# Feature-on-partition products with one 512-wide moving operand for both halves of the activation, group by group

## The chip, the core and the metric

The kernel runs on one core of a Trainium2 chip. The metric is the device time of one execution in microseconds, taken as the median of several runs. The core has a matrix engine (TensorE, PE in the profile; its weight loads are listed apart as PEld), a vector engine (VectorE, DVE), a scalar engine (ScalarE, ACT), GpSimd (POOL), and SyncE (SP), which only issues transfers here. Each engine runs its own instructions in the order in which they were written, and waits on semaphores for the others. Products land in PSUM banks of 128 partitions x 512 floats; everything else lies in SBUF.

## What is computed

Three layers on one sequence of 256 rows and 1024 features, all in float32. The first two are mixer plus MLP, the third is a hybrid of attention and convolution:

```
# layers 1 and 2
x = x + rmsnorm(mixer(rmsnorm(x, g0)), g1)          # HGRN2 + retention; then mLSTM
x = x + rmsnorm(square(relu(rmsnorm(x, g2) @ w1)) @ w2, g3)   # w1: 1024 x 4096
# layer 3
h = rmsnorm(x, g) * (1 + scale) + shift             # shift, scale, gate from silu(c) @ w_ada
q, k, v, g_attn, cb, cc, cx, g_conv, m_attn, m_conv = split(h @ w_in)   # 10 x 1024 columns
y_attn = (attention(q, k, v) * silu(g_attn)) @ w_o_attn
y_conv = (cb * conv(cc * cx) * silu(g_conv)) @ w_o_conv
out = rmsnorm(x + gate * ((sigmoid(m_attn) * y_attn + sigmoid(m_conv) * y_conv) @ w_out), final_g)
```

## The kernel before

Every large product is made exact enough by halves: an operand a is kept as hi (rounded to the format that PE multiplies in one pass, fp32r) and lo = a - hi, and a product is hi x hi + hi x lo + lo x hi, three matmuls that add up in one PSUM bank. Weights come from memory as raw tiles of 128 x 1024 floats (512 KB, five buffers, tag `raw`). Each is split into a **unit** (`u`, hi and lo, eight buffers): ACT copies raw to hi, DVE subtracts hi from raw for lo (`emit_split`). Most units hold 256 rows of a weight matrix by 512 columns.

There are two kinds of product.

- **A** (`mmA`, `blockA`, `stagA`, `out_stag`, `w2_block`): the activation is the stationary operand (128 x 128), the weights move with 512 columns, and rows of the sequence land on the partitions.
- **B** (`mmB`, `blockB`): the weights are stationary (128 x 128), the activation moves with its 256 rows, and features land on the partitions. A B block makes 512 output features from four units; its two banks hold two groups of 128 features each. There are 38 such blocks: two in the first mixer, six in each MLP, two in the second mixer, 22 in the third layer.

`blockB` goes unit by unit: for each unit, its two contraction steps `a`, and in each step the four groups `c`; `mmB` issues three matmuls of 256 columns. When the last unit is done, `evac(ps)` gets both banks. In the MLPs the banks come from the ring `ax` (four), elsewhere from `mm` (four). In the MLPs a B block is followed by a `w2_block` of kind A. The activations lie in the class `Act`: one tile for all hi, one for all lo, as [T, k, 128] (`tk`) or [k, 256] (`kt`).

What stands where in the program is decided by a planner at build time (`Sched`). It keeps one clock for each engine from cost figures given with each operation (109.0 ns for a B matmul, 216.3 for an A matmul), and starts pieces of other work ("jobs", generators that yield) between matmuls when their inputs should be ready. `pump` emits loads and splits ahead of their use, as long as raw and unit buffers are free; each unit has a due time from the sum of the costs that stand with `U(...)`.

Users of B blocks that the change touches: `evac_b` (relu squared in the MLPs), `l3_q`, `l3_k` and `attn` (attention), `conv_half`, `gate_block`, and `wo_conv`, whose activation was two four-step halves joined by `Both`. The first mixer's first B block (`ev_f`) follows a `stagA` stage; around it DVE and ACT also do a small softmax (`vec_job`), and DVE multiplies by the gain vector `ghg`, which is loaded late. In attention a head is scores (PE), then bias, maximum, exponential, sum and scaling (DVE, ACT), then transposes (PE), a copy (ACT), and the product with v (PE), all as a job between the matmuls of B blocks.

Of the kernel before, what the change touches and what calls it, by code (L numbers as in the profile page):

```python
# [34 lines left out]
LAST = -1.0  # L35
# [158 lines left out]
class Both:  # L194
    def __init__(self, a, b):
        self.a = (a, b)

    def r(self, i, kt):
        return self.a[kt // 4].r(i, kt % 4)
# [3 lines left out]
def tile_model(ctx: ExitStack, tc: tile.TileContext, I: dict, out: bass.AP, stop=None):  # L203
# [294 lines left out]
    def blockB(w, c0, act, evac, alloc=None, nk=8):  # L498

        us = units1(w, c0, 0, nk)  # L500
        ps = []

        def fn(j):
            def g(u):
                if j == 0:
                    ps.extend([(alloc or mmb)(), (alloc or mmb)()])
# [29 lines left out]
    def new_act8():  # L536
        return Act(a8(F32R), a8(F32R), "tk", 8)

# [43 lines left out]
    class Stage:  # L582
# [6 lines left out]
        def get(self):  # L589
            if self.act is None:  # L590
                self.act = new_act8()
# [432 lines left out]
    def mlp(l, stage, nxt, gpost, gpre, shift=None, ada=None):  # L1024
# [26 lines left out]
        def evac_b(b):  # L1051
            def evac(ps):
                def job():
                    Z[b] = z_tile(b)
                    for i in range(2):
                        r, s_ = s2(), s2()
                        A(r, ps[i], AF.Relu)
                        tt(s_, r, r, ALU.mult)
                        hi, lo = (Z[b].p[k][:, 2 * i:2 * i + 2, :].rearrange("p k c -> p (k c)") for k in range(2))
                        A(hi, r, AF.Square)  # L1060
# [385 lines left out]

    def l3_g(b):
# [10 lines left out]
    def l3_q(b):  # L1458
        def evac(ps):
            E3["q", b] = s4()  # L1460
            for i in range(2):
                A(E3["q", b][:, i * 512:i * 512 + 512], ps[i], AF.Copy, scale=128.0 ** -0.5)
        return evac

    def l3_k(b):
        def evac(ps):
            if b == 0:
                E3["oT"] = Act(a8(F32R), a8(F32R), "kt", 8)
            prev = E3.get("att")
            E3["att"] = sc.start(attn(b, prev, ps))  # L1470
        return evac

    def attn(b, prev, ps):
        E3["k", b] = s4()
# [305 lines left out]
```

## Time and profile before

| what | us |
|---|---|
| median of 3 runs | 989.31 (987.98 to 989.83) |
| the profiled execution | 986.43 |
| its span, first to last instruction | 984.6 |
| PE busy in the span | 967.7 |
| DVE busy | 669.8 |
| ACT busy | 541.1 |

The profiled execution is one run; its rows add up to its span, and 1.8 us lie outside the span. Busy times of an engine are unions, so a matmul whose drain overlaps the next counts once there, while "mean ns of one" includes the overlap. The pace of a stream is therefore read from the starts of successive pieces, not from that mean.

### The profile page before, as it was taken

To read this page: it belongs to the slowest core of one execution; us is meant where nothing else is said; L and a number is where in the kernel's file an instruction comes from. 1 tells how busy PE (TensorE), PEld (TensorE's weight loads), DVE (VectorE), ACT (ScalarE), POOL (GpSimd) and SP (SyncE) were. 2 spreads that over 40 slices of the span, in tenths; PEclk is the share of its full clock that TensorE was granted. 3 is DMA by queue.
4 is the path that set the end of the run, shared out by engine and by line. 5 is a ranking of instruction groups with operands and counts; after the bars stand their busy time and mean duration, and the time that the engine had idled before them with its cause. 6 is when DMAs were issued, how large, how long until landed. Compare 5 with 4: busy or idle time off the path is not lost.

```text
span 984.6 us, 15496 instructions
## 1 busy us (share of the span) xinstructions
PE 967.7 (98%) x6168; PEld 874.6 (89%) x6168; DVE 669.8 (68%) x885; ACT 541.1 (55%) x772; POOL 4.1 (0%) x11
## 2 busy tenths in 40 slices
PE   8999999999999999998999999999999999999997
PEld 6998888789989987987799999988999999999995
DVE  6689776775555547787888878658545577546564
ACT  7663565764554446766656544646545446444533
POOL 1000000000000000000000000000000000000000
PEclk9999999999999999999999999999999999999999
DMA  8670447566766546546679987626874426865531
GB/s 310 219 243 22 150 150 271 159 202 201 233 183 195 172 120 203 166 139 213 206 252 338 332 286 260 182 90 219 235 231 129 136 80 203 267 188 178 189 111 43
DMA packets 84316, 189.71 MB, mean 193 GB/s; under 512 B 7184, under 2 KB 9616, under 8 KB 84244
## 3 DMA queue, kind: packets, MB, share of 16 engines
q1 hardware_dynamic: 83956, 188.21, 59.8%
q8 instruction: 48, 0.79, 0.3%
q10 hardware_dynamic: 288, 0.52, 0.1%
q14 instruction: 24, 0.20, 0.1%
HBM read 187.46 MB, written 1.25 MB: 192 GB/s over the span
## 4 chain that ended last, share of the span: by engine, by line
PE 86%; DVE 7%; ACT 3%; issue 2%; DMA 2%; SPq 0%; DVEq 0%; ACTq 0%
PE mm L291 66%; PE ax L291 19%; DVE u L264 3%; DVE s L275 2%; PE ax L295 2%; DMA x<-in_x_dram 1%; ACT junk L260 1%; DMA raw<-in_mlp_w_dram 1%; DVE s L264 1%; DVE x L264 1%; ACT u L260 0%; SPq L306 0%; ACT s L260 0%; ACT L260 0%; DVE a L264 0%
## 5 line engine op out<-in xcount | busy, mean ns | idle before, releaser
L264 DVE TENSOR_TENSOR u<-raw,u 128x1024 fp32r<-128x1024 f32 x316 | 380.4, 1222 | 195.4 <-ACT u L260 194.2
L291 PE MATMUL mm<-u,a 128*128 128x512 f32 x1968 | 469.3, 394 | 4.5 <-ACT a L260 2.0
L260 ACT ACTIVATE u<-raw 128x1024 fp32r<-128x1024 f32 x316 | 328.6, 1055 | 230.7 <-PE mm L291 128.7
L291 PEld LDWEIGHTS mm<-u,a 128*128 128x128 f32 x1968 | 364.7, 188 | 83.1 <-DVE a L264 3.5
L291 PE MATMUL mm<-a,u 128*128 128x256 f32 x2496 | 305.3, 284 | 0.0
L291 PEld LDWEIGHTS mm<-a,u 128*128 128x128 f32 x2496 | 301.5, 192 | 0.6
L291 PEld LDWEIGHTS ax<-a,u 128*128 128x128 f32 x1152 | 139.9, 192 | 0.9
L291 PE MATMUL ax<-a,u 128*128 128x256 f32 x1152 | 140.6, 283 | 0.0
L260 ACT ACTIVATE s<-mm 128x512 f32<-128x512 f32 x64 | 36.4, 592 | 25.9 <-PE mm L291 25.1
L260 ACT ACTIVATE s<-ax 128x512 f32<-128x512 f32 (+1 forms) x43 | 24.5, 570 | 44.3 <-PE ax L295 23.6
L279 DVE RECIPROCAL sm<-sm 128x1 f32<-128x1 f32 (+2 forms) x43 | 7.0, 164 | 57.0 <-ACT sm L260 48.2
L260 ACT ACTIVATE a<-s 128x512 fp32r<-128x512 f32 (+1 forms) x37 | 23.8, 644 | 22.9 <-DVE s L264 22.1
L260 ACT ACT_TABLE_LOAD x27 | 34.6, 1283 | 2.3 <-DVE lbv L264 0.9
L264 DVE TENSOR_TENSOR s<-mm,s 128x512 f32<-128x512 f32 (+1 forms) x46 | 27.8, 637 | 12.0 <-PE mm L291 7.7
L295 PE MATMUL ax<-ident,s 128*128 128x128 f32 (+1 forms) x196 | 29.8, 273 | 4.4 <-DVE s L264 3.2
L295 PEld LDWEIGHTS ax<-ident,s 128*128 128x128 f32 (+1 forms) x196 | 23.1, 140 | 11.1 <-issue 4.4
L260 ACT ACTIVATE a<-ax 128x512 fp32r<-128x512 f32 x38 | 22.2, 595 | 19.1 <-PE ax L295 18.7
L264 DVE TENSOR_TENSOR a<-s,a 128x512 fp32r<-128x512 f32 x36 | 24.9, 692 | 11.3 <-ACT a L260 8.8
L264 DVE TENSOR_TENSOR s<-s,s 128x512 f32<-128x512 f32 (+4 forms) x42 | 28.9, 691 | 2.8 <-ACT s L260 2.0
L264 DVE TENSOR_TENSOR a<-ax,a 128x512 fp32r<-128x512 f32 x38 | 25.6, 686 | 7.1 <-ACT a L260 7.1
L291 PE MATMUL ax<-s,s 128*128 128x256 f32 (+2 forms) x156 | 29.9, 331 | 0.0
L275 DVE SCALAR_TENSOR_TENSOR s<-raw,silc,s 128x1024 f32<-128x1024 f32 x21 | 26.9, 1279 | 0.0
(98 smaller groups left out, 353.2 us busy)
## 6 DMA issues: line engine op xcount, KB each, us to landing
raw<-in_mlp_w_dram SPq DMA_DIRECT2D x128, 512.0 KB
raw<-in_w_in_dram SPq DMA_DIRECT2D x80, 512.0 KB
raw<-in_ev_w_in_dram SPq DMA_DIRECT2D x40, 512.0 KB
raw<-in_od_w_in_dram SPq DMA_DIRECT2D x24, 512.0 KB
raw<-in_w_ada_dram SPq DMA_DIRECT2D x24, 512.0 KB
raw<-in_ev_w_out_dram SPq DMA_DIRECT2D x12, 512.0 KB
s<-in_norm_g_dram SPq DMA_DIRECT2D x8, 512.0 KB
raw<-in_od_w_out_dram SPq DMA_DIRECT2D x8, 512.0 KB
```

Source lines behind the costliest of these rows:

```text
L260: nc.scalar.activation(o, i, f, **kw)
L264: (nc.vector if e == "v" else nc.gpsimd).tensor_tensor(out=o, in0=a, in1=b, op=op)
L275: nc.vector.scalar_tensor_tensor(out=o, in0=a, scalar=s, in1=b, op0=op0, op1=op1, **kw)
L279: nc.vector.reciprocal(o, i)
L291: nc.tensor.matmul(o, l, r, start=start, stop=stop_)
L295: nc.tensor.transpose(o, i, idt)
```

## The change

`Act` stays for the last product and for intermediate activations of kind A; a new class `Pair` replaces it (and `Both`) where B blocks read. It stores hi and lo of the same contraction step side by side, in tiles of four steps each, so that `both(kt)` is one operand of 512 columns: hi of 256 rows, then lo of 256 rows. `mmB` issues one matmul of 512 columns (hi weights against both halves, which fills a whole bank: hi x hi in its first 256 columns, hi x lo in the others) and one of 256 (lo weights against hi, into the first 256). `blockB` runs group by group: each of the four column groups has a bank of its own and runs through all four units. When a group ends, `hi_lo_sum` copies the second half of its bank to SBUF (ACT) and adds the first half (DVE). The evacuations then read sums in SBUF; those that were plain copies (q, k, cc) are gone, and the gates are taken in place. The factor of q moved into the DVE step that adds the bias to the scores. `evac_b` squares on DVE in the first MLP and on ACT in the second.

```
 class Pair:
+    def __init__(self, lay, tiles):
+        ...
+        form = "p (t k i c) -> p t k i c" if lay == "tk" else "p (k i c) -> p k i c"
+        dims = dict(t=2, k=4, i=2) if lay == "tk" else dict(k=4, i=2)
...
+    def both(self, kt):
+        p, k = self.p[kt // 4], kt % 4
+        if self.lay == "tk":
+            return p[:, :, k, :, :].rearrange("p t i c -> p i t c")
+        return p[:, k, :, :].rearrange("p i c -> p (i c)")
...
     def mmB(ps, act, kt, u, off, start, stop_):
         wh, wl = u[:, 0, off:off + 128], u[:, 1, off:off + 128]
-        mm(ps, wh, act.r(0, kt), start, False, 109.0)
-        mm(ps, wh, act.r(1, kt), False, False, 109.0)
-        mm(ps, wl, act.r(0, kt), False, stop_, 109.0)
+        if stop_:
+            mm(ps[:, 0:256], wl, act.r(0, kt), False, False, 120.0)
+        o = ps.rearrange("p (i t c) -> p i t c", i=2, t=2) if act.lay == "tk" else ps
+        mm(o, wh, act.both(kt), start, stop_, 226.5)
+        if not stop_:
+            mm(ps[:, 0:256], wl, act.r(0, kt), False, False, 120.0)
...
-    def blockB(w, c0, act, evac, alloc=None, nk=8):
+    def blockB(w, c0, act, evac, alloc=None, into=None):
...
+                if j == 0:
+                    ps[c] = (alloc or mmb)()
                 for a in range(2):
-                    for c in range(4):
-                        mmB(ps[c // 2][:, (c % 2) * 256:(c % 2) * 256 + 256], act(), 2 * j + a, u,
-                            a * 512 + c * 128, j == 0 and a == 0 and c % 2 == 0, j == nk // 2 - 1 and a == 1 and c % 2 == 1)
+                    mmB(ps[c], act(), 2 * j + a, u, a * 512 + c * 128, j == 0 and a == 0, j == 3 and a == 1)
             return g
-        for j in range(nk // 2):
-            U(us[j], fn(j), 2620.0)
-        F(lambda: evac(ps))
+        def add(c):
+            def f():
+                if c == 0 and into is not None:
+                    t = into()
+                    vs.extend([t[:, 0:512], t[:, 512:1024]])
+                elif c % 2 == 0 and into is None:
+                    vs.append(s2())
+                o = (c % 2) * 256
+                jobs.append(sc.start(hi_lo_sum(vs[c // 2][:, o:o + 256], ps[c], c == 3)))
+                if c == 3:
+                    for j in jobs:
+                        sc.finish(j)
+                    evac(vs)
+            return f
+
+        for c in range(4):
+            for j in range(4):
+                U(us[j], fn(c, j), 693.0)
+            F(add(c))
+
+    def hi_lo_sum(o, ps, now):
+        if not now:
+            yield
+        A(o, ps[:, 256:512])
+        if not now:
+            yield
+        tt(o, ps[:, 0:256], o, ALU.add)
+        yield LAST
...
-                        r, s_ = s2(), s2()
-                        A(r, ps[i], AF.Relu)
-                        tt(s_, r, r, ALU.mult)
+                        s_ = s2()
+                        if ada is None:
+                            stt(s_, ps[i], 0.0, ps[i], ALU.max, ALU.mult)
+                        else:
+                            A(s_, ps[i], AF.Relu)
+                            A(s_, s_, AF.Square)
...
-            tt(L[:, 0:128], sp[:, 0:128], bt[:, h, 128:256], ALU.add)
-            tt(L[:, 128:384], sp[:, 128:384], bt[:, h, :], ALU.add)
+            stt(L[:, 0:128], sp[:, 0:128], 128.0 ** -0.5, bt[:, h, 128:256], ALU.mult, ALU.add)
+            stt(L[:, 128:384], sp[:, 128:384], 128.0 ** -0.5, bt[:, h, :], ALU.mult, ALU.add)
...
-        blockB(w_in, 512 * b, y_in.get, l3_q(b))
-        blockB(w_in, 1024 + 512 * b, y_in.get, l3_k(b))
+        blockB(w_in, 512 * b, y_in.get, lambda ps: None, into=keep(("q", b)))
+        blockB(w_in, 1024 + 512 * b, y_in.get, l3_k(b), into=keep(("k", b)))
```

The instructions move as follows. On PE, at the start of the first mixer's first B block, before (`mm` banks, `u` units, `a` activation tiles; the numbers tell buffers apart):

```order
L291 MATMUL mm_368<-a_13_123,u_302 128x256 [waits Activation_49]
L291 MATMUL mm_368<-a_14_124,u_302 128x256
L291 MATMUL mm_368<-a_13_123,u_302 128x256 [waits DVE_49]
...
L291 MATMUL mm_369<-a_13_123,u_302 128x256 x2
L291 MATMUL mm_369<-a_14_124,u_302 128x256
...
L291 MATMUL mm_368<-a_13_123,u_337 128x256 [waits Activation_49]
L291 MATMUL mm_368<-a_14_124,u_337 128x256
L291 MATMUL mm_368<-a_13_123,u_337 128x256 [waits DVE_49]
```

and in the changed kernel:

```order
L319 MATMUL mm_373<-a_13_123,u_302 128x512 [waits Activation_49]
L319 MATMUL mm_373<-a_13_123,u_302 128x256 [waits DVE_49]
...
L319 MATMUL mm_373<-a_13_123,u_313 128x512 [waits Activation_49]
L319 MATMUL mm_373<-a_13_123,u_313 128x256 [waits DVE_49]
...
L319 MATMUL mm_373<-a_14_124,u_318 128x512 [waits Activation_49]
L319 MATMUL mm_373<-a_14_124,u_318 128x256 [waits DVE_49]
...
L319 MATMUL mm_373<-a_14_124,u_347 128x512 [waits Activation_49]
L319 MATMUL mm_373<-a_14_124,u_347 128x256 [waits DVE_49]
...
L319 MATMUL mm_391<-a_13_123,u_302 128x512
```

The second unit (u_337 before, u_313 now) is first read after 24 matmuls before and after four now, and the block's first bank reads all four units before its second bank begins.

On DVE around the small softmax of `vec_job` (`sm`, `vec`, `lbv`, `silc`), just ahead of that block, before:

```order
L264 TENSOR_TENSOR s_48_269<-s_48_269,ghg 128x512 [waits DMAHW0_49,DVE_49]
L264 TENSOR_TENSOR u_302<-raw_172,u_302 128x1024 [waits DMAHW5_49,Activation_49]
L264 TENSOR_TENSOR sm_318<-vec 128x4 [waits Activation_49]
...
L270 TENSOR_SCALAR lbv<-lbv 128x4 [waits DVE_49]
L264 TENSOR_TENSOR silc<-vec,sm_317 128x8 [waits Activation_49]
L264 TENSOR_TENSOR u_337<-raw_182,u_337 128x1024 [waits DMAHW6_49,PE_49,Activation_49]
L264 TENSOR_TENSOR u_354<-raw_205,u_354 128x1024 [waits DMAHW7_49,PE_49,Activation_49]
```

and in the changed kernel:

```order
L292 TENSOR_TENSOR s_48_269<-s_48_269,ghg 128x512 [waits DMAHW0_49,DVE_49]
L292 TENSOR_TENSOR u_302<-raw_172,u_302 128x1024 [waits DMAHW5_49,Activation_49]
L292 TENSOR_TENSOR u_313<-raw_182,u_313 128x1024 [waits DMAHW6_49,Activation_49]
L292 TENSOR_TENSOR u_318<-raw_205,u_318 128x1024 [waits DMAHW7_49,Activation_49]
L292 TENSOR_TENSOR sm_328<-vec 128x4 [waits Activation_49]
...
L292 TENSOR_TENSOR silc<-vec,sm_327 128x8 [waits Activation_49]
L292 TENSOR_TENSOR u_347<-raw_215,u_347 128x1024 [waits PE_49,Activation_49]
```

Two more splits stand ahead of the softmax now, and the block's fourth unit is the first behind it. ACT has its part in the same order: the hi copy of that unit comes after the second table load of the softmax.

On DVE in the third layer, around the first head of the second half of the heads (`s` from `ax`: scores plus bias), before:

```order
L264 TENSOR_TENSOR u_7211<-raw_6977,u_7211 128x1024
L264 TENSOR_TENSOR s_1079_7235<-ax_7232,a_987_6391 128x128
L264 TENSOR_TENSOR s_1079_7235<-ax_7232,a_987_6391 128x256
L287 TENSOR_REDUCE sm_7236<-s_1079_7235 128x1 x2
L270 TENSOR_SCALAR sm_7236<-sm_7236 128x2
```

and in the changed kernel:

```order
L292 TENSOR_TENSOR s_1115_6604<-mm_6587,s_1115_6604 128x256
L292 TENSOR_TENSOR u_6646<-raw_6506,u_6646 128x1024
L292 TENSOR_TENSOR u_6657<-raw_6515,u_6657 128x1024
L303 SCALAR_TENSOR_TENSOR s_1131_6678<-ax_6675,a_1025_6000 128x128
L303 SCALAR_TENSOR_TENSOR s_1131_6678<-ax_6675,a_1025_6000 128x256
L315 TENSOR_REDUCE sm_6679<-s_1131_6678 128x1 x2
L298 TENSOR_SCALAR sm_6679<-sm_6679 128x2
```

The sum of a group's two halves (the 128x256 row that reads `mm_6587`) and two splits stand ahead of the head's chain, where one split stood. Between this head's scores and its transposes PE has 18 matmuls of its B blocks in the changed kernel (nine of 512 and nine of 256), and 34 of 256 before.

## Rows read from the trace of the kernel before

**Rows 1.** The page: span, and busy time of each engine.
```profile
span 984.6 us, 15496 instructions
...
PE 967.7 (98%) x6168; PEld 874.6 (89%) x6168; DVE 669.8 (68%) x885; ACT 541.1 (55%) x772; POOL 4.1 (0%) x11
```
**Rows 2.** The page: the chain that ended last, shares by engine.
```profile
PE 86%; DVE 7%; ACT 3%; issue 2%; DMA 2%; SPq 0%; DVEq 0%; ACTq 0%
```
**Rows 3.** The chain from 223 to 258: start us, us, what (first MLP).
```profile
223.79 10.91 PE mm L291 x48
234.70 11.51 PE ax L291 x96
246.21 10.91 PE mm L291 x48
```
**Rows 4.** Costliest groups: xcount, busy us, mean ns of one, idle before.
```profile
L291 PE MATMUL mm<-a,u 128*128 128x256 f32 x2496 | 305.3, 284 | 0.0
...
L291 PE MATMUL ax<-a,u 128*128 128x256 f32 x1152 | 140.6, 283 | 0.0
```
**Rows 5.** Busy time of each engine in one B block, then clock, DMA share, GB/s.
```profile
234.55:246.05 11.50, 11.50 (x97) 11.50 (x96) 4.90 (x4) 4.23 (x4) 0.00 (x0) 1.00 0.71 213
```
**Rows 6.** The chain from 394 to 398: gate products, 36 weight columns, 256 moving.
```profile
394.53 2.77 PE ax L291 x24
```
**Rows 7.** PE busy in 20 us of tk blocks, and of kt blocks.
```profile
812.00:832.00 20.00, 20.00 (x169) 1.00 0.62 189
...
934.00:954.00 20.00, 20.00 (x169) 1.00 0.47 157
```
**Rows 8.** Timeline from 27 to 40, around the first B block's start.
```profile
28.96 0.69 DVE L264 TENSOR_TENSOR s<-s,ghg 128x512 f32<-128x512 f32 x1 [4.13 <-DMA ghg<-in_ev_hg_norm_g_dram]
...
29.57 1.22 DVE L264 TENSOR_TENSOR u<-raw,u 128x1024 fp32r<-128x1024 f32 x1
...
33.80 1.99 ACT L260 ACTIVATE u<-raw 128x1024 fp32r<-128x1024 f32 x2
...
34.36 5.92 PE L291 MATMUL mm<-a,u 128*128 128x256 f32 x48
34.87 2.36 DVE L264 TENSOR_TENSOR u<-raw,u 128x1024 fp32r<-128x1024 f32 x2 [0.78 <-ACT u L260]
```
**Rows 9.** Timeline from 504 to 507: the second MLP's first B block.
```profile
504.17 2.35 DVE L264 TENSOR_TENSOR u<-raw,u 128x1024 fp32r<-128x1024 f32 x2
...
505.36 1.83 PE L291 MATMUL ax<-a,u 128*128 128x256 f32 x14
```
**Rows 10.** Costliest groups, two rows; then engines' busy time from 700 to 800.
```profile
L264 DVE TENSOR_TENSOR s<-mm,s 128x512 f32<-128x512 f32 x38 | 25.1, 685 | 12.0 <-PE mm L291 7.7 <-ACT s L260 4.3
...
L260 ACT ACTIVATE junk<-ax 128x256 f32<-128x256 f32 x12 | 4.6, 385 | 5.8 <-PE ax L291 5.7
...
700.00:800.00 100.00, 100.00 (x819) 99.31 (x819) 55.44 (x98) 49.99 (x84) 0.00 (x0) 1.00 0.57 162
```
**Rows 11.** Timeline from 745 to 756: one head of attention.
```profile
746.96 0.49 ACT L260 ACTIVATE s<-ax 128x384 f32<-128x384 f32 x1 [2.76 <-PE ax L295]
...
749.20 4.77 PE L291 MATMUL mm<-a,u 128*128 128x256 f32 x37
749.59 0.62 DVE L264 TENSOR_TENSOR s<-ax,a 128x128 f32<-128x128 f32 x2
...
752.19 0.55 DVE L270 TENSOR_SCALAR s<-s,sm 128x128 f32<-128x128 f32 x2
```
**Rows 12.** Timeline from 451 to 462: PE's longest idle inside the program.
```profile
457.70 1.17 PE L295 MATMUL ax<-ident,s 128*128 128x128 f32 x8 [2.87 <-DVE s L264]
```
**Rows 13.** Timeline from 955 to 962: the last stage's start.
```profile
955.82 6.54 PE L291 MATMUL mm<-u,a 128*128 128x512 f32 x28
...
960.74 0.69 DVE L264 TENSOR_TENSOR a<-s,a 128x512 fp32r<-128x512 f32 x1 [0.70 <-ACT a L260]
```
**Rows 14.** Busy times in a stretch of the second MLP; the last two: DMA share, GB/s.
```profile
528.53:539.74 11.21, 11.21 (x96) 11.21 (x95) 9.18 (x8) 6.04 (x7) 0.00 (x0) 1.00 0.98 362
```

More of the change, by code (lines that the diff above doesn't have):

```diff
@@ L537, in new_act8, with new_pair8 @@
         return Act(a8(F32R), a8(F32R), "tk", 8)
+    def new_pair8(lay="tk"):
+        return Pair(lay, [a8(F32R), a8(F32R)])
     def to_act(src, act, T, k0, n):
@@ L590, in get @@
             if self.act is None:
-                self.act = new_act8()
+                self.act = new_pair8()
             return self.act
@@ L1445, in silu_fm, with keep, f @@
             tt(dst[:, c], ps[i], dst[:, c], ALU.mult)
+    def keep(key):
+        def f():
+            E3[key] = s4()
+            return E3[key]
+        return f
     def l3_g(b):
@@ L1456, in tile_model @@
         blockB(w_in, 3072 + 512 * b, y_in.get, l3_g(b))
[L1458 to L1463, printed above, removed]
     def l3_k(b):
@@ L1467, in evac, with attn @@
             if b == 0:
-                E3["oT"] = Act(a8(F32R), a8(F32R), "kt", 8)
+                E3["oT"] = new_pair8("kt")
             prev = E3.get("att")
-            E3["att"] = sc.start(attn(b, prev, ps))
+            E3["att"] = sc.start(attn(b, prev))
         return evac
-    def attn(b, prev, ps):
-        E3["k", b] = s4()
-        for i in range(2):
-            A(E3["k", b][:, i * 512:i * 512 + 512], ps[i])
+    def attn(b, prev):
         yield
@@ L1515, in attn @@
                 tt(ob, po, E3["g", b][:, (hh - 1) * 256:(hh + 1) * 256], ALU.mult)
-                hi, lo = (E3["oT"].p[i][:, h - 1:h + 1, :].rearrange("p k c -> p (k c)") for i in range(2))
+                hi, lo = (E3["oT"].f(i, h - 1, 2) for i in range(2))
+                ob = ob.rearrange("p (k c) -> p k c", k=2)
                 A(hi, ob)
@@ L1529, in cc @@
         def cc(ps):
-            K["u"] = s4()
-            for i in range(2):
-                A(K["u"][:, i * 512:i * 512 + 512], ps[i])
+            K["u"] = E3["u", b]
         def cx(ps):
@@ L1570, in job @@
                     k0 = 2 * i
-                    hi, lo = (act.p[n][:, k0:k0 + 2, :].rearrange("p k c -> p (k c)") for n in range(2))
-                    A(hi, g[:, c])
-                    tt(lo, g[:, c], hi.bitcast(F32), ALU.subtract)
+                    hi, lo = (act.f(n, k0, 2) for n in range(2))
+                    g3 = g[:, c].rearrange("p (k c) -> p k c", k=2)
+                    A(hi, g3)
+                    tt(lo, g3, hi.bitcast(F32), ALU.subtract)
                 yield LAST
@@ L1577, in conv_half @@
         for o, f in ((5120, cc), (6144, cx), (4096, cb), (7168, cg)):
-            blockB(w_in, o + 512 * b, y_in.get, f)
+            blockB(w_in, o + 512 * b, y_in.get, f, into=keep(("u", b)) if f is cc else None)
     def gate_block(key, o):
@@ L1582, in evac @@
             def evac(ps):
-                E3[key, b] = s4()
                 for i in range(2):
-                    A(E3[key, b][:, i * 512:i * 512 + 512], ps[i], AF.Sigmoid)
+                    A(ps[i], ps[i], AF.Sigmoid)
             return evac
         for b in range(2):
-            blockB(w_in, o + 512 * b, y_in.get, mk(b))
+            blockB(w_in, o + 512 * b, y_in.get, mk(b), into=keep((key, b)))
     def wo_attn(b):
```

35 lines of the change are left out of this document (23 added, 12 removed).

## The prediction

> **What bounds the kernel now.** I read the page's busy shares first: TensorE (PE) is busy 967.7 us of a span of 984.6 us, the vector engine (DVE) 68% and the scalar engine (ACT) 55% [rows 1]. The chain that ended last says the same: 86% of it is PE [rows 2]. So the time is PE's stream, and an edit pays if it shortens that stream or opens no new hole in it. PE's 16.9 us of idle lie mostly at the start and the end; between them one stall of 2.87 us in the second layer's mixer stands out, and comes up below.
>
> Next I took the chain over one piece of the MLP, where two kinds of stage alternate, so that the start of a piece to the start of the next is the pure pace. Activation-stationary products of 512 columns: 48 from 223.79 to 234.70, 10.91 us, 227.3 ns each. Feature-on-partition products (the kind the change touches, "B" below) of 256 columns: 96 from 234.70 to 246.21, 11.51 us, 119.9 ns each [rows 3]. The granted clock is 2.4 GHz there (1.00 of full speed), so 512 columns are 213.3 ns and 256 are 106.7: the pair of weight load and matmul costs 14.0 and 13.2 ns beyond its columns. There are 2496 + 1152 = 3648 such 256-column matmuls [rows 4], which is 38 B blocks of 96, or 1216 groups of three (one contraction step of one output bank).
>
> **The change part by part.** *The matmuls.* A group was hi x hi, hi x lo, lo x hi, three times 256 columns. It becomes one matmul of 512 (hi weights against both halves) and one of 256: the same 768 columns, one pair less. By the pure paces 3 x 119.9 = 359.7 ns becomes 227.3 + 119.9 = 347.2, so 12.5 ns a group and 1216 x 12.5 = 15.2 us in all. No row shows the two widths alternating, so both ends need a bound. Upper gain: if the weight load were wholly hidden behind the wide matmul, only columns remain, 768 / 2.4 = 320 ns, 39.7 ns a group, 48 us. Weight loads are busy 11.50 of 11.50 us in a B block [rows 5], which leaves that possible; but the stream of 24 gate products with only 36 weight columns still takes 2.77 us, 115.4 ns each, 8.7 beyond its columns [rows 6], so a shorter load takes away a third of the excess, not all. If both matmuls of a group paid only those 8.7 ns, a group would be 337.4 and the gain 22.3 ns, 27 us: there I put the upper end. Lower end: nothing saved, or a loss, if the wide moving operand is read more slowly than a plain one; in the stage layout it is four separate runs of 128 now, two before. Blocks with runs of 128 and blocks with one run of 256 keep the same pace, 169 matmuls touched in 20 us each [rows 7], so I expect no price. I take 12.5 because the pure 512 stream already has its load hidden behind a long matmul and still shows 14.0.
>
> Against that stands a rule: the Trainium skill, TensorE: Matmul & The Clock Gate, section "Back-to-back issue gap", gives a warm matmul N / 2.4 + 2.5 ns; by it a pair less would save 2.5 ns, 3.0 us in all. The rows measured here are 13 to 14 ns above the columns, not 2.5, and I follow them.
>
> *The order.* Before, a B block went unit by unit (a unit is 256 rows of weights, split into hi and lo by ACT and DVE) through all four column groups, so its four units were wanted 2.9 us apart. Now each column group runs through all four units, which are wanted 0.69 us apart (4 steps of 173.6 ns). The splits have to be ready some 6.6 us earlier for the last unit, and the buffers come free only in the block's last quarter. I compared split ends with the new due times. It fails in the first block, in the first mixer. There DVE is held by a gain vector's transfer until 28.96, splits the first unit from 29.57 to 30.79, then does a small softmax with ACT; the next unit's hi copy starts on ACT at 33.80, 3.0 us later, and its lo ends at 36.0, with PE in the block since 34.5 [rows 8]. In the changed order units 2 and 3 are split ahead of that softmax and only the fourth behind it. So: 30.79 + 2 x 1.15 = 33.1, + 3.0 = 36.1 for its hi copy, 37.2 when that ends, + 1.3 = 38.5 for its lo. PE wants the hi at 34.5 + 12 x 0.174 = 36.6 and the lo a matmul later: it waits 0.6 and then 1.0 us, **1.7 us** together with the signals.
>
> The next tightest I found is the first B block of the second MLP: the fourth unit's split ends at 505.3 and it is wanted 2.3 us after the block's start at 505.5, so 2.5 us are left [rows 9]. Elsewhere I read 4 us or more. In the order of the changed kernel no other unit's split stands behind a PE result that ends later than 36 matmuls (about 7 us) before the unit's use. Cost nothing; the cover is the eight unit buffers, and without it a late split would cost its own 1.2 us.
>
> *The adds.* Each bank now ends in an ACT copy of 256 and a DVE add of 256, four of each a block: about 0.39 us by the 256-wide ACT row and 0.35 by half the 512-wide DVE row. In the last layer DVE is busy 55.44 us of 100 and ACT 50 [rows 10], and 1.4 and 1.5 us per 11 us block fit; and ACT's copies of q, k and u go. In the MLPs one DVE square a half becomes a fused step or an ACT square. Hidden. They also stand in the queue ahead of attention, whose scores are now scaled in the same DVE step as the bias. There the chain from scores to transposes is what PE waits for: scores issued until 749.20, DVE from 749.59 to 752.74, so 3.6 us from the next PE issue [rows 11]. In the changed order PE has 3.12 us of matmuls in that place for one head, 3.8 to 7.3 for the other seven (4.1 before at the least): 0.5 us of stall. Between transposes and the product with v one place shrinks from 1.32 to 0.69 us, against 0.28 + 0.49 us for the ACT copy [rows 11] and a signal: 0.2 us. I take 1.0 us for attention, 0.7 at the least, and 8 x 1.23 = 10 us if a split stood in front of each head's chain.
>
> The 2.87 us stall in the second mixer [rows 12] ends a DVE chain that starts at the end of the k block. The adds lengthen it by 0.8 us, but the convolution now starts ahead of two splits (2.4 us) that it stood behind, and the scores are issued four matmuls later. I take 0, plus or minus 1.5. At the end, the last half of the merged activation is complete at 961.4 and PE wants it 36 matmuls of 227.3 ns after 955.95, at 964.1 [rows 13]; 1.1 us of added steps stay hidden.
>
> *Sum.* -15.2 + 1.7 + 1.0 = -12.5 us: span 984.6 to 972.1, and with the 1.8 us outside it 986.4 to 973.9 for the profiled execution. The median shown is 989.31, 2.9 above that execution; 989.3 - 12.5 = 976.8, **977.0**. No more than 0.2% (2 us) can be told from no change.
>
> **The rivals.** *More is hidden.* 22.3 ns a group go: -27.1 + 2.7, 964.9. For it: the loads are the busiest row in a B block; against it, the 512 stream. *Supply breaks.* Where the second MLP also streams the 24 conditioning matrices, DMA engines are 0.98 busy [rows 14]; the unit buffers now come free in bursts, the five raw buffers fill and the transfers pause. A 22 us period needs 12 loads of 512 KB, 1.45 us each at the 362 GB/s of that row, so PE waits only if they pause over 4.6 us of it. With 1 to 2 us of such wait in five periods it is 982 to 987. Against it: the unit that now has 2.5 us left was 9 us early before, and the later ones there no less. *Nothing is saved per pair*: the excess belongs to the columns (119.9 / 256 each), the wide matmul takes 239.8: 989.3 + 2.7 = 992.0. Against it: 227.3 in the rows. The page's 2.5 ns would put 989.0 in the same case. *The other side.* The wide moving operand of four runs is slower in 36 of the 38 blocks (1152 groups). Beyond (15.2 - 2.7) / 1152 = 10.9 ns each the gain is gone; at 20 ns it is 989.3 - 12.5 + 23 = 999.8. Against it: the equal pace of one and two runs.
>
> **How the numbers follow.** Forecast 0.70 (971 to 982), more hidden 0.10, supply 0.11, nothing saved 0.05, slower operand 0.04. Faster by over 0.2%: 0.70 + 0.10 + 0.08 of supply = 0.88. Within: 0.03 of supply and 0.03 of nothing saved = 0.06. Slower: 0.02 + 0.04 = 0.06. The range leaves out the last two cases, the worst of supply and the best of more hidden: 968 to 985.
>
> **What would show it.** Right: B blocks of 11.1 us (64 matmuls) in the chain where 11.51 stood, 1216 matmuls and as many weight loads less, one hole of about 1.7 us near 37 us, DVE up by some 45 us. Wrong: a B block at 10.6 or 11.5 us; PE idle in the MLPs ended by a raw transfer; idle ahead of the transposes of most heads.

## The result and the profile after

The changed kernel takes **993.74 us** (991.94 to 995.45), against 988.43 for the kernel before on the same chip: a ratio of **1.0055 [1.0035, 1.0075]**. It is slower by 0.55%, 5.4 us, where I forecast 977.0 and gave slower a chance of 0.06.

The page of after, beside [rows 1, 2, 4]; busy time and share, then the chain that ended last:

```profile
span 993.7 us, 13327 instructions
PE 965.7 (97%) x4952; PEld 813.5 (82%) x4952; DVE 710.2 (71%) x1025; ACT 581.4 (59%) x912; POOL 4.2 (0%) x11
...
PE 78%; DVE 12%; ACT 5%; issue 3%; DMA 2%; SPq 0%; DVEq 0%; ACTq 0%
...
L319 PE MATMUL mm<-a,u 128*128 128x512 f32 (+1 forms) x1664 | 301.1, 342 | 2.5 <-DVE s L292 0.9
...
L319 PE MATMUL ax<-a,u 128*128 128x512 f32 (+1 forms) x768 | 138.0, 339 | 0.0
```

The 1216 matmuls are gone, 1664 + 768 = 2432 remain of 3648, and DVE is busier by 40 us. But PE's share of the chain fell from 86% to 78%, and DVE's rose to 12%: PE has fewer matmuls and new holes. Its busy time fell by 2.0 us, and its idle time rose from 16.9 to 28.0.

Where the 9.1 us between the two profiled spans lie (kinds A and B as above; starts of the stages taken from PE's order of time):

| stretch | before | after | difference |
|---|---|---|---|
| opening, up to the first B block | 34.36 | 35.84 | +1.5 |
| two B blocks of the first mixer | 23.03 | 24.72 | +1.7 |
| rest of the first mixer | 154.29 | 154.07 | -0.2 |
| first MLP, and the stage behind it | 185.46 | 183.92 | -1.5 |
| two B blocks of the second mixer | 23.56 | 23.35 | -0.2 |
| rest of the second mixer | 84.66 | 89.92 | **+5.3** |
| second MLP, and the stage behind it | 184.16 | 182.54 | -1.6 |
| 22 B blocks of the last layer | 266.30 | 268.47 | **+2.2** |
| last product and the end | 28.78 | 30.87 | **+2.1** |

The opening stands ahead of every changed block, and differs with the clock that its first 20 us were granted: over all kernels here the first B block starts at 34.2 to 34.9 where that was 1.00, as in before, at 34.6 to 35.9 where it was 0.91, as in after, and at 36.2 to 36.7 where it was 0.83. The two profiled runs lie 9 us apart, the medians 5.3, because the one of before was below its median and the one of after above.

What PE waited for in after, the three longest in total (total, times, longest):

```profile
PE mm L319 <- DVE u L292: 5.7, 5, 3.8
PE ax L323 <- DVE s L292: 2.7, 2, 2.4
PE mm L319 <- ACT a L288: 2.7, 2, 1.6
```

First in the list now stands a split (`u`) that DVE had not made in time; before, splits held PE up for 1.0 us in all.

### The profile page after: what moved, and what is told of

Its sections match the earlier page's. It is cut to its first block, busy times and chain, and to the rows that moved or that the text cites. A ratio compares the mean times of both kernels' runs of the same rounds, so it can differ in the third digit from the quotient of the medians.

```text
span 993.7 us, 13327 instructions
## 1 busy us (share of the span) xinstructions
PE 965.7 (97%) x4952; PEld 813.5 (82%) x4952; DVE 710.2 (71%) x1025; ACT 581.4 (59%) x912; POOL 4.2 (0%) x11
## 4 chain that ended last, share of the span: by engine, by line
PE 78%; DVE 12%; ACT 5%; issue 3%; DMA 2%; SPq 0%; DVEq 0%; ACTq 0%
PE mm L319 58%; PE ax L319 18%; DVE u L292 5%; DVE s L303 3%; DVE s L292 2%; ACT u L288 2%; PE ax L323 2%; ACT s L288 1%; DMA x<-in_x_dram 1%; DVE a L292 1%; ACT junk L288 1%; ACT L288 1%; DMA raw<-in_ev_w_in_dram 1%; DVE x L292 1%; SPq L334 0%
## 5 line engine op out<-in xcount | busy, mean ns | idle before, releaser
L319 PE MATMUL mm<-a,u 128*128 128x512 f32 (+1 forms) x1664 | 301.1, 342 | 2.5 <-DVE s L292 0.9
L319 PEld LDWEIGHTS mm<-a,u 128*128 128x128 f32 x1664 | 256.8, 189 | 41.4 <-ACT u L288 1.2
L319 PE MATMUL ax<-a,u 128*128 128x512 f32 (+1 forms) x768 | 138.0, 339 | 0.0
L319 PEld LDWEIGHTS ax<-a,u 128*128 128x128 f32 x768 | 118.6, 188 | 18.0
L288 ACT ACTIVATE s<-mm 128x256 f32<-128x256 f32 (+1 forms) x136 | 57.9, 430 | 95.5 <-PE mm L319 95.3
L288 ACT ACTIVATE s<-ax 128x256 f32<-128x256 f32 (+2 forms) x67 | 28.8, 430 | 83.7 <-PE ax L319 66.5
L292 DVE TENSOR_TENSOR s<-mm,s 128x256 f32<-128x256 f32 (+1 forms) x126 | 52.7, 446 | 14.6 <-ACT s L288 8.8
L292 DVE TENSOR_TENSOR s<-s,s 128x512 f32<-128x512 f32 (+4 forms) x66 | 44.5, 689 | 8.7 <-ACT s L288 7.9
L288 ACT ACTIVATE s<-s 128x512 f32<-128x512 f32 (+3 forms) x62 | 37.5, 616 | 2.7 <-DVE s L292 1.8
L292 DVE TENSOR_TENSOR s<-ax,s 128x256 f32<-128x256 f32 (+2 forms) x60 | 26.3, 459 | 14.8 <-ACT s L288 11.3
L288 ACT ACT_TABLE_LOAD x27 | 34.6, 1283 | 2.1 <-DVE lbv L292 0.9
```

Source lines behind the costliest of these rows:

```text
L288: nc.scalar.activation(o, i, f, **kw)
L292: (nc.vector if e == "v" else nc.gpsimd).tensor_tensor(out=o, in0=a, in1=b, op=op)
L319: nc.tensor.matmul(o, l, r, start=start, stop=stop_)
```

## Experiments

Each kernel is the changed one with one edit; ratios are to the kernel before, which is 987 to 988 us.

**The pair by itself.** The wide matmul is taken apart again; order and sums stay.

```
-        mm(o, wh, act.both(kt), start, stop_, 226.5)
+        mm(ps[:, 0:256], wh, act.r(0, kt), start, False, 113.25)
+        mm(ps[:, 256:512], wh, act.r(1, kt), False, stop_, 113.25)
```

> The changed kernel, with the 512-wide matmul of each group split again into two of 256 (same weights, same bank, same place); order, splits, sums and the planner's figures stay, so nothing but the pair of weight load and matmul comes back. Theory: the pair was worth 7.4 ns a group (B block 11.27 us against 11.51), and the rest of what was lost lies in the queues of DVE and ACT. Then B blocks go back to 11.5 us, the stall in the second mixer shrinks only by the two blocks ahead of it (3.8 to about 3.3), and the time is 1000 to 1003. Rival, the pair saves nothing and the shorter blocks have another cause: 993 to 995, blocks of 11.27. Rival, the holes come from PE being faster: the time stays near 994 with blocks of 11.5, and the holes of the last layer (5 us) go.

1001.15 us, 1.0138 [1.0122, 1.0153]. One B block of the MLP, in after, in this kernel, and with the turned order of the next experiment (the stretch, PE, PEld, DVE, ACT, POOL, the granted clock, DMA):

```profile
237.24:248.51 11.27, 11.27 (x65) 9.81 (x64) 4.15 (x6) 3.61 (x6) 0.00 (x0) 1.00 0.64 236
```
```profile
236.17:247.68 11.51, 11.51 (x97) 11.51 (x96) 4.17 (x6) 3.62 (x6) 0.00 (x0) 1.00 0.65 238
```
```profile
236.14:247.29 11.15, 11.15 (x66) 9.73 (x65) 4.17 (x6) 3.56 (x6) 0.00 (x0) 1.00 0.65 244
```

Taken apart, the block is at the 11.51 of before [rows 5] with the same DVE and ACT work. So the wide matmul is worth 0.24 us a block, 11.27 / 32 = 352.2 ns a group against 359.7: 7.5 ns, 9.1 us in 38 blocks, and 8.2 us of the measured time (1.0138 to 1.0055). All the rest of the change (order, sums, the steps that moved with them), with the old matmuls, costs 13.6 us. No run here takes the order and the sums apart. The second mixer's stall was 3.74 us here too, where I expected 3.3: a PE that is 2% slower does not cover it. In attention three of the four holes of after became smaller (0.52, 0.69 and 0.67 for 0.78, 0.93 and 0.91) and the longest stayed (1.88), so the faster PE made them only in small part.

**Turning every other step.** Odd contraction steps issue the narrow matmul first.

```
-        if stop_:
+        if kt % 2:
             mm(ps[:, 0:256], wl, act.r(0, kt), False, False, 120.0)
...
-        if not stop_:
+        if not kt % 2:
```

> The changed kernel, with the two matmuls of each odd contraction step issued narrow first, so that the stream of a bank reads wide, narrow, narrow, wide instead of wide, narrow, wide, narrow; everything else alike. Theory: the 5 ns by which a group (352.3) is above the sum of the two pure paces (347.2) are paid where the width changes, and halving the changes gives back half: blocks of 11.19 us instead of 11.27, about 3 us in all, 990 to 992. Rival: they belong to the wide matmul with its operand from two tiles, or to the narrow one behind it: blocks of 11.27, 993 to 995.

990.60, 1.0036 [1.0023, 1.0049]; blocks of 11.15 (third fence above), 348.4 ns a group. Of the 5.0 ns by which a group stood above the two pure paces, 3.8 go with the order of the widths. They are not a price per change of width. The last step of each bank was narrow first in after already, so 14 changes a bank became eight, and at that price none at all would give 343.3, below the 347.2 of the pure streams. And in the block of after shown above a step to the next start is as long where the width stays as where it changes: 234.7 and 235.3 ns behind a wide matmul, 116.5 and 117.1 behind a narrow one (but only seven steps of the first kind). Over 38 blocks the turn shortens the stream by 4.6 us and the time by 3 (medians), 2 (ratios). In the MLPs all of it arrives (1.5 us in 12 blocks); the holes in the second mixer (3.78) and in attention (4.49 us in sum, for 4.50) stayed as long as in after. Where the remainder went, no run shows.

**The planner's clock.** Two kernels change only cost figures, and thereby the order.

```
-            mm(ps[:, 0:256], wl, act.r(0, kt), False, False, 120.0)
+            mm(ps[:, 0:256], wl, act.r(0, kt), False, False, 109.0)
...
-        mm(o, wh, act.both(kt), start, stop_, 226.5)
+        mm(o, wh, act.both(kt), start, stop_, 218.0)
...
-                U(us[j], fn(c, j), 693.0)
+                U(us[j], fn(c, j), 654.0)
```

> The changed kernel, with the planner's cost figures of a group put back from 346.5 to the 327 that stood before (218 and 109, and 654 for a unit's share of a block); the instructions are the same, only their order may move. Before, PE ran 10% behind the planner's clock in B blocks (359.7 ns a group against 327), now 1.6% (352 against 346.5). Theory, that this lag was what kept DVE and ACT ahead of PE: the holes in attention (0.78, 0.93, 1.88, 0.91), and some of those in the second mixer and the tail, go: 983 to 989. Rival, the holes come from the work that now stands in the queues of DVE and ACT, at whatever distance: 991 to 996.

998.19, 1.0112 [1.0088, 1.0136]: slower still. The second edit adds 80 ns to the figures of three helpers, `A` (ACT) and `tt` and `stt` (most of DVE's work): `fs(i) / 1.2 + 90` to `+ 170`, `+ 70` to `+ 150`:

> The changed kernel, with 80 ns more in the planner's figures for each ACT and DVE instruction, which is what they miss in the trace (DVE 1024 wide 1220 ns against 1137, 256 wide 417 against 337; ACT 1024 wide 1052 against 943, 256 wide 380 against 303). Order alone may move. Theory of the lost lag: this puts the cover back from the other side, 984 to 990, with the attention holes gone. Rival, the queue's content decides: 991 to 996. It could also go up, if sums and evacuations are now issued so late that PE waits for banks: above 997.

994.18, 1.0074 [1.0057, 1.0091], not told apart from the changed kernel. PE in the last layer of the first, then of the second of these:

```profile
810.97 4.62 PE L319 MATMUL mm<-a,u 128*128 128x512 f32 x16 [4.45 <-DVE s L292]
838.38 3.89 PE L319 MATMUL mm<-a,u 128*128 128x512 f32 x12 [2.05 <-DVE s L292]
```
```profile
809.98 4.73 PE L319 MATMUL mm<-a,u 128*128 128x512 f32 x25 [2.52 <-DVE s L292]
835.83 6.33 PE L319 MATMUL mm<-a,u 128*128 128x512 f32 x26 [2.04 <-DVE s L292]
```

In both, the holes ahead of the transposes are gone, and larger ones stand in their place, where a new column group waits for a sum to release its bank. My theory of the lost lag falls: moving the planner's clock moves the holes and does not remove them.

**The second mixer's two blocks undone.** `block3` is the old `blockB` with the old `mmB` (two banks, no sums).

```
-    blockB(w_od, 0, o_in.get, od_qk("q", 0, 1.0))
+    block3(w_od, 0, o_in.get, od_qk("q", 0, 1.0))
...
-    blockB(w_od, 512, o_in.get, od_k_evac)
+    block3(w_od, 512, o_in.get, od_k_evac)
```

> The changed kernel, with the two feature-on-partition blocks of the second mixer (its q and k) as they were before: three matmuls of 256 a group, unit by unit, no sums, the convolution reading the banks. Theory: the 3.77 us stall there (DVE's queue holds four sums and the k convolution ahead of the two splits that PE wants), with the lower granted clock behind it, is 5.3 us of the 9.1 lost, and comes from these two blocks: it falls to 0.3, the two blocks give back 0.5 us of pace, and the time is 988.5 to 989.5. Rival, the stall is handed down from the stages ahead (planner, transfers): it stays above 2 us and the time at 992 to 995.

989.20, 1.0024 [1.0012, 1.0036]. PE behind the k block, in after and here, and two stretches of five us in after (the last three figures: granted clock, DMA share, GB/s):

```profile
434.38 5.30 PE L319 MATMUL mm<-u,a 128*128 128x512 f32 x12 [3.77 <-DVE u L292]
```
```profile
429.23 2.13 PE L319 MATMUL mm<-u,a 128*128 128x512 f32 x8 [0.33 <-DVE u L292]
```
```profile
430.00:435.00 5.00, 1.23 (x5) 0.72 (x4) 5.00 (x11) 4.95 (x7) 0.00 (x0) 0.75 0.29 120
435.00:440.00 5.00, 5.00 (x15) 3.94 (x14) 1.75 (x3) 2.44 (x5) 0.00 (x0) 0.57 0.64 210
```

The stall and what follows it are local to these blocks: the rest of the mixer is 85.48 us again. In after, the hole was followed by a granted clock of 0.57 over five us, most of them at the 1.2 GHz level, and 12 matmuls of 512 took 5.13 us from the first start to the start behind them (439.51) instead of 12 x 227.3 ns = 2.73.

**Work taken out of DVE's queue.** The eight gate-mask steps wait until k's convolution is done.

```
-            while not sj.done:
+            while not sj.done or ("kjob", 1) not in E2 or not E2["kjob", 1].done:
                 yield 200.0
```

> The changed kernel, with the eight gate-mask steps of DVE in the second mixer (2.72 us, 421.34 to 424.06) moved behind the convolution of k; the sums, the splits and the convolution stay. Theory: the 3.77 us stall is the length of DVE's queue from the end of the k block to the split PE wants, so it falls by the 2.7 taken out, to 1.0 or 1.1, and the two matmul stretches behind it keep the clock longer; the masks then stand ahead of the scores' product, and the later stall of 2.36 grows by up to 2.7. Time 990 to 994. Rival: the stall is set by ACT's convolution steps or by the transfers of the units, not by the amount of work in DVE's queue: it stays above 3 us.

990.46, 1.0027 [1.0015, 1.0038]. DVE in after, from the masks to the two splits PE waits for; then DVE and PE in this kernel:

```profile
421.34 2.72 DVE L303 SCALAR_TENSOR_TENSOR s<-s,col,s 128x256 f32<-128x256 f32 x8
423.97 1.22 DVE L292 TENSOR_TENSOR u<-raw,u 128x1024 fp32r<-128x1024 f32 x1
425.11 0.42 DVE L292 TENSOR_TENSOR s<-mm,s 128x256 f32<-128x256 f32 x1
425.44 1.22 DVE L292 TENSOR_TENSOR u<-raw,u 128x1024 fp32r<-128x1024 f32 x1
426.57 0.42 DVE L292 TENSOR_TENSOR s<-mm,s 128x256 f32<-128x256 f32 x1
426.91 1.22 DVE L292 TENSOR_TENSOR u<-raw,u 128x1024 fp32r<-128x1024 f32 x1
428.04 0.42 DVE L292 TENSOR_TENSOR s<-mm,s 128x256 f32<-128x256 f32 x1
428.37 4.81 DVE L303 SCALAR_TENSOR_TENSOR s<-s,vec,s 128x253 f32<-128x253 f32 x12
433.10 2.36 DVE L292 TENSOR_TENSOR u<-raw,u 128x1024 fp32r<-128x1024 f32 x2
```
```profile
423.21 4.82 DVE L303 SCALAR_TENSOR_TENSOR s<-s,vec,s 128x253 f32<-128x253 f32 x12
427.94 2.37 DVE L292 TENSOR_TENSOR u<-raw,u 128x1024 fp32r<-128x1024 f32 x2
```
```profile
429.22 4.15 PE L319 MATMUL mm<-u,a 128*128 128x512 f32 x17 [1.29 <-DVE u L292]
```

DVE never idles between 420.2 and 435.5 in after. Taking 2.7 us of other work out of that queue takes 2.5 out of the stall. The stall is the length of DVE's queue, not ACT's steps or a transfer. The later stall did not grow as I expected (2.15 and 0.62 us, for 2.36 and 0.36 in after), but the lower clock now came behind it: 0.53 from 455 to 460. So the rest of the mixer gave back 1.9 us (88.00 against 89.92), not 2.5.

**Sums into the queues at once**, in all 38 blocks.

```
-    def blockB(w, c0, act, evac, alloc=None, into=None):
+    def blockB(w, c0, act, evac, alloc=None, into=None, now=True):
...
-                jobs.append(sc.start(hi_lo_sum(vs[c // 2][:, o:o + 256], ps[c], c == 3)))
+                jobs.append(sc.start(hi_lo_sum(vs[c // 2][:, o:o + 256], ps[c], now or c == 3)))
```

> The changed kernel, with each sum (ACT copy, DVE add) put into its queues as soon as its column group's last matmul is issued, instead of some hundred ns later by the planner's clock, in all 38 blocks. Theory, that the place of the sums in the queues decides: banks come free earlier and the last evacuation of a block has no sums ahead of it, so the bank wait at 838.75 (0.91 us) goes and the second mixer's stall shrinks by 1 us or more; against that a split behind a sum waits for its matmul; 988 to 993 if the first weighs more, 996 or more if splits come late in the MLPs. Rival, the sums' own work is the load and not their place: 993 to 995.

989.26, 1.0016 [1.0003, 1.0030]. PE's waits of over 0.1 us in the last layer's B stretch, in after and here:

```profile
781.59 0.70 PE L323 MATMUL ax<-ident,s 128*128 128x128 f32 x3 [0.78 <-DVE s L298]
797.39 0.70 PE L323 MATMUL ax<-ident,s 128*128 128x128 f32 x3 [0.93 <-DVE s L298]
813.53 0.92 PE L319 MATMUL ax<-s,s 128*128 128x256 f32 x4 [1.88 <-ACT s L288]
838.75 1.51 PE L319 MATMUL mm<-a,u 128*128 128x512 f32 x7 [0.91 <-DVE s L292]
```
```profile
810.11 0.70 PE L323 MATMUL ax<-ident,s 128*128 128x128 f32 x3 [0.73 <-DVE s L298]
811.79 0.96 PE L319 MATMUL mm<-a,u 128*128 128x256 f32 x4 [0.75 <-DVE u L292]
```

Four holes of 4.5 us become two of 1.5, and the stretch falls from 268.47 to 263.29: here it is the place of the sums in the queues, not their work. Some 1.7 us of the 5.2 are the clock, which stayed at 1.00 from 800 to 820 (0.91 in after). The second mixer's stall stayed (3.79), against what I expected: there the same work stands ahead of the split wherever the sums are.

**Attention's q and k blocks undone.**

```
-        blockB(w_in, 512 * b, y_in.get, lambda ps: None, into=keep(("q", b)))
-        blockB(w_in, 1024 + 512 * b, y_in.get, l3_k(b), into=keep(("k", b)))
+        block3(w_in, 512 * b, y_in.get, copy(("q", b)))
+        block3(w_in, 1024 + 512 * b, y_in.get, l3_k(b))
```

> The changed kernel, with the four q and k blocks of the last layer as they were before (three matmuls of 256 a group, unit by unit, no sums; q and k copied from the banks by ACT); the scale of the scores stays in the DVE step. Theory: the stalls of the feature-on-partition stretch of the last layer, 7.4 us with the lower clock behind them (781.59, 797.39, 813.53, 838.75), come from the sums and the crowded splits of these four blocks and from PE having too little to do between a head's scores and its transposes; undone they go, less 4 x 0.24 us of pace: the stretch from 571.5 us of the layer's work falls from 268.5 to about 262, the time from 993.7 to 987.3. Rival: they come from the sums of the other blocks and from the scale in DVE, which both stay: two or more of the four holes stay, 991 or more.

992.48, 1.0051 [1.0038, 1.0064], not told apart from the changed kernel: the rival's time, though not its holes. Those at 781, 797 and 813 go, so they did come from these four blocks; one of 1.28 us comes at the first head, and of two bank waits ended by DVE's sums one stays (0.91) and one comes (0.71), from the other blocks. The stretch is 265.82, not 262.

**The gain vector's transfer first.**

```
     def small_loads():
+        load(ghg, I["ev_hg_norm_g"][0].partition_broadcast(128))
         ...
-        load(ghg, I["ev_hg_norm_g"][0].partition_broadcast(128))
```

> The changed kernel, with the transfer of the gain vector on which DVE waits in the first mixer (it landed at 30.7 in the profiled run of the changed kernel, 28.5 in the run whose second mixer was undone, where the first block had no hole) issued ahead of the vectors' and masks' transfers instead of behind them; nothing else moves. Theory: the holes of 0.87 and 0.76 us in the first feature-on-partition block hang on that landing: with DVE free 2 us sooner they go, 991.5 to 993. Rival: they come from the small softmax between the third and the fourth split alone, and stay: 993 to 995.

992.72, 1.0052 [1.0033, 1.0071], a gain too small for the time to show, but the trace does. DVE's step on that vector and the fourth unit's split, in after and here, and the two holes of PE in after:

```profile
30.78 0.70 DVE L292 TENSOR_TENSOR s<-s,ghg 128x512 f32<-128x512 f32 x1 [4.53 <-DMA ghg<-in_ev_hg_norm_g_dram]
...
38.97 1.23 DVE L292 TENSOR_TENSOR u<-raw,u 128x1024 fp32r<-128x1024 f32 x1 [0.78 <-ACT u L288]
```
```profile
27.87 0.69 DVE L292 TENSOR_TENSOR s<-s,ghg 128x512 f32<-128x512 f32 x1 [1.12 <-DMA ghg<-in_ev_hg_norm_g_dram]
...
36.50 1.23 DVE L292 TENSOR_TENSOR u<-raw,u 128x1024 fp32r<-128x1024 f32 x1 [0.79 <-ACT u L288]
```
```profile
38.98 0.50 PE L319 MATMUL mm<-a,u 128*128 128x512 f32 x1 [0.87 <-ACT u L288]
40.24 0.97 PE L319 MATMUL mm<-a,u 128*128 128x256 f32 x4 [0.76 <-DVE u L292]
```

With the vector there 2.9 us sooner (the first B block began only 0.4 later), PE has no hole in that block, and the two B blocks take 22.56 us instead of 24.72. The second mixer's and attention's holes are the same as in after.

**Blocks chosen by place.** Nine blocks as before (first mixer's first, second mixer's two, attention's four, the last convolution's output projection's two), 29 changed, with `block3` as above:

> The changed kernel, with nine of its 38 feature-on-partition blocks as before: the first of the first mixer, the two of the second mixer, the four q and k of the last layer, the two of its convolution's output projection. 29 blocks keep the wide matmul, the order by column groups and the sums. Theory, that each loss is local to the queue of its place: 993.7 less 4.8 (second mixer, measured), less 6.4 (attention), less 2.1 (the tail) and up to 1.7 (the first block), plus 3 x 0.24 for the blocks not yet counted: 979 to 981, below the kernel before by 7 to 9. Rival, the lost time moves on to the next tight place (the blocks behind, whose units are now wanted at other times): 985 to 990.

983.55, 0.9966 [0.9954, 0.9978]: faster than before, by 4 us, though not by the 8 expected; the last layer's stretch gave 2.2 us of the 6.4 (266.29): as with attention alone undone, the 1.28 us at the first head and two bank waits (0.72 and 0.92) are there. The end is back at 21.95 us for the last product (23.98 in after). Next, five blocks as before (attention's changed again), sums at once, odd steps turned:

> Five of the 38 blocks as before (the first of the first mixer, the two of the second mixer, the two of the last convolution's output projection), the other 33 with the wide matmul, column groups and sums, each sum put into its queues at once (as in the run with immediate sums), and odd contraction steps issued narrow first (as in the run with the turned order). If the gains and losses found one by one are local and add up: the run with immediate sums, 989.3, less 4.8 (second mixer), less 1.3 (tail) and 0.8 (first block), plus 5 x 0.24, less 33 x 0.125 x 0.8: 978 to 982, faster than the kernel before by 6 to 10 us. Rival, a faster PE only lengthens waits whose ends DVE and ACT set: the turned order gives nothing on top, 983 to 986.

981.52, **0.9935 [0.9921, 0.9949]**. The sum of the single runs was 980.3, so gains and losses found one by one add up within 1.2 us. And with attention's four undone too:

> The fastest kernel so far (five blocks as before, sums at once, odd steps narrow first), with the four q and k blocks of the last layer as before too, so that 29 blocks keep the change. Theory, that the two holes left in attention there (1.77 us ended by DVE's softmax steps, 0.75 us by a split, and a clock of 0.91 behind them, some 4 us together) come from the units of these four blocks being wanted in a bunch while DVE does the softmax: they go, against 4 x 0.37 us of pace: 979 to 980, the last layer's stretch from 263.7 to 261.5. Rival, a head's chain through DVE and ACT is as long in either order and one hole of 1 to 2 us stays: 981 to 983.

980.23, 0.9929 [0.9915, 0.9942], not told apart from the one ahead. The hole of 1.77 shrank to 0.35 and that of 0.75 stayed, but the 1.28 at the first head came back, and the stretch is 263.98: as the rival said, holes of over 1 us stay in either style. Both kernels beat before and after.

## Why the prediction was wrong, step by step

Term by term, forecast and then what the two profiled spans show (each loss with the pace that its blocks should have gained): matmuls -15.2 and -9.1 us; first block +1.7 and +2.2; second mixer 0 and +5.3; attention +1.0 and +7.4; the end 0 and +2.1. With 1.5 for the opening, that is the 9.1 of the table within some tenths. The first term was the right mechanism at the wrong size; what turned a gain into a loss are the terms for work in DVE's and ACT's queues that I put at nothing or nearly so.

**The matmuls: right mechanism, wrong size.** I took 12.5 ns a group from two pure streams; it was 7.5. The alternating stream costs more than the sum of its parts, and I had said that no row shows it. 9.1 us were saved, not 15.2. Layout made no difference, as forecast: a block with four runs and one with a single run take 11.27 and 11.28 us (928.99 to 940.26 and on to 951.54). The blocks of four runs are 34, not the 36 that the rival on the wide operand counts. An estimate by the Trainium skill's rule (TensorE: Matmul & The Clock Gate, "Back-to-back issue gap"), which the page gives for a matmul by itself and not for a stream of pairs with weight loads, is 3.0 us; the block with the pair and the block without show 9.1.

**The first block: right.** 1.7 us forecast, holes of 0.87 and 0.76 measured, at 37 to 40 us, from the split behind the small softmax [rows 8]. I began from the landing of the vector at 28.96; the run with its transfer first shows that the holes hang on it: where it lands early they are gone.

**The second mixer: where it failed most.** I took 0 for the convolution, which "now starts ahead of two splits (2.4 us) that it stood behind", and looked only at who waits for the convolution [rows 12]. That reading of the order was wrong. The same two splits stand behind the convolution in both kernels, and the first of them is the one for which PE waits. DVE in before, and PE at that split:

```profile
421.37 2.35 DVE L264 TENSOR_TENSOR u<-raw,u 128x1024 fp32r<-128x1024 f32 x2
423.64 4.76 DVE L275 SCALAR_TENSOR_TENSOR s<-mm,vec,s 128x253 f32<-128x253 f32 x12
428.32 2.35 DVE L264 TENSOR_TENSOR u<-raw,u 128x1024 fp32r<-128x1024 f32 x2
```
```profile
429.58 2.14 PE L291 MATMUL mm<-u,a 128*128 128x512 f32 x8 [0.31 <-DVE u L264]
```

What changed stands ahead of the convolution. Between q's convolution and k's, DVE's queue holds six splits and four sums in after, five splits and no sum in before. So k's convolution starts 6.5 us after the block's end (428.37 against 421.90), where it was 2.9 (423.64 against 420.70), and the split behind it is as much later. That is 3.77 us of hole instead of 0.31, and 5.3 in all with the clock behind it. By the lengths of these steps (about 1.1 us a split, 0.34 a sum) some 1.4 us of the 3.5 are the sums, and 1.1 the split, which in before was made ahead of q's convolution (401.30). The stall I did watch hardly moved: 2.36 + 0.36, for 2.87.

**Attention: half seen.** "0.5 us of stall" ahead of the transposes was 0.78 and 0.93. The 0.2 us at the copy was 1.88: on ACT the copy stood behind the hi copies of three splits and three sum copies. The bank wait (0.91) I had not thought of; a bank is now released by a sum, and this one stood behind three splits. ACT in after ahead of that copy, and DVE ahead of those sums, beside [rows 11]:

```profile
809.35 2.00 ACT L288 ACTIVATE u<-raw 128x1024 fp32r<-128x1024 f32 x2
811.25 0.35 ACT L288 ACTIVATE s<-mm 128x256 f32<-128x256 f32 x1
811.51 1.04 ACT L288 ACTIVATE u<-raw 128x1024 fp32r<-128x1024 f32 x1
812.46 0.63 ACT L288 ACTIVATE s<-mm 128x256 f32<-128x256 f32 x2
812.99 0.49 ACT L288 ACTIVATE s<-ax 128x384 f32<-128x384 f32 x1
```
```profile
834.77 3.50 DVE L292 TENSOR_TENSOR u<-raw,u 128x1024 fp32r<-128x1024 f32 x3 [0.53 <-ACT u L288]
838.18 1.41 DVE L292 TENSOR_TENSOR s<-mm,s 128x256 f32<-128x256 f32 x4
```

The stretch should have been 266.30 - 22 x 0.24 = 261.0 and was 268.5. The holes are 4.5 of these 7.4 us, and a clock of 0.91 from 800 to 820 some 1.8. The other 1.1 us are, by an estimate, what a stop costs beside the idle time that the rows list: the three transposes behind a hole take 0.70 us (781.59, 797.39) where they take 0.49 without one (788.71), and the matmul ahead of a hole runs out some 0.16 past its pace. The places I looked at cost 3.6 us (0.78, 0.93, 1.88) for the 1.0 I took; this lies inside my bounds of 0.7 and 10. The mechanism of the upper bound, a split in front of a head's chain on DVE, stands ahead of the hole at 781.59 (two splits, from 776.30 to 778.65), but most heads have no hole.

**The tail: hidden, I said.** The merged activation was in time. But the last units' splits stood on DVE behind the steps that merge it; in before the last split was made from 961.69 and PE had no hole [rows 13], in after the last two are made from 971.40 while PE waits. DVE in before, then DVE and PE in after:

```profile
961.69 1.23 DVE L264 TENSOR_TENSOR u<-raw,u 128x1024 fp32r<-128x1024 f32 x1 [0.26 <-ACT u L260]
```
```profile
971.40 2.36 DVE L292 TENSOR_TENSOR u<-raw,u 128x1024 fp32r<-128x1024 f32 x2 [0.26 <-ACT u L288]
```
```profile
971.42 0.49 PE L319 MATMUL mm<-u,a 128*128 128x512 f32 x1 [0.27 <-ACT u L288]
972.68 0.96 PE L319 MATMUL mm<-u,a 128*128 128x512 f32 x3 [0.76 <-DVE u L292]
973.81 1.42 PE L319 MATMUL mm<-u,a 128*128 128x512 f32 x5 [0.17 <-DVE u L292]
```

The three stops are 1.20 us of idle, and the stretch is 2.1 longer; the kernels with these blocks undone have no hole there.

**"Cost nothing" for splits elsewhere** is the common root, and the step that failed. I looked for a PE result ahead of a split in its queue, and summed DVE's and ACT's work over a block (1.4 and 1.5 us "fit"). I did not go through what else stands in the queue between a sum and the next split at the three places where DVE was already full: masks and convolution, a head's softmax, the merge. In the MLPs the work did fit: no new hole in their 12 B blocks, each shorter by just the pace, though in the second DVE also works on the conditioning matrices and is busy 15.9 us of 20 (540 to 560). So a high busy share alone did not make a hole; work in the queue just ahead of a split did. The supply rival, priced there, did not happen, and the rival that ended on the other side named the wrong mechanism: a group stood 5.0 ns above the two pure paces, not 20, and most of that went with the order of the widths.

## What to carry to other kernels

An order that makes the units of a block due in a bunch, with added steps on the engines that make them, is paid where those engines are full already, so list for each such place what stands in the queue ahead of the step that the bottleneck waits for, not only whether busy shares leave room. Average slack (DVE 68%) says nothing about a stretch in which it runs 15 us without a break. And a change that gains in most blocks and loses at a few places is worth applying block by block: the kernel that keeps 29 of 38, with nothing else altered, is 0.34% faster than before, the one that changes all 0.55% slower. With the sums at once and the turned order besides, the one that keeps 33 is 0.65% faster.

## What the hardware showed that I had not expected

A stream that alternates 512 and 256 columns takes 352.2 ns a group where the pure streams add up to 347.2; in the order wide, narrow, narrow, wide it is 348.4. Why the order of the widths matters stays open.

A hole can cost more than itself, and not always: behind 3.77 us the granted clock was 0.57 for five us, while around and behind the 2.87 us of before it stayed 1.00 from 440 to 480. With the same 2.87 us at the same place in the kernel whose second mixer was undone it was 0.67 from 455 to 460. In attention the same four holes came with 0.91 from 800 to 820 in after, and with 1.00 in the kernel with the gain vector first, whose stretch was 1.5 us shorter (266.94).
